# Gated convolution input with tokens on partitions, turned back to channels by three VectorE block transposes a group and quadrant transfers inside SBUF

## The chip, the cores and the metric

The kernel runs on one core of a Trainium2 chip. The metric is device time in microseconds (us), from the first to the last instruction of one execution; "median" is that of several executions. The core has a matrix engine (PE, called TensorE), a vector engine (DVE, VectorE), a scalar engine (ACT, ScalarE), a fourth engine (POOL, GpSimd) and the SyncE queue (SP), which here issues nearly all transfers (DMAs). Each engine works through its own instructions strictly in the order in which the program was built; an instruction that has to wait holds back everything behind it on its engine. The same holds for SP: a transfer that has to wait holds back those behind it.

## What is computed

One layer of a streaming encoder for 384 tokens (256 of a prompt, 8 streams of 16): a normed projection `w_in`, a conformer convolution branch, an attention branch, a gated mix, and a ConvGLU feed-forward part. The part that matters here is the input of the convolution branch and its state:

```python
h = rmsnorm(x, norm_mix_g)
proj = h @ w_in
glu_in = proj[..., :o0]                        # 2 * D_CONV = 2048 columns: values, then gates
u = glu_in[..., :D_CONV] * jax.nn.sigmoid(glu_in[..., D_CONV:])
ext = jnp.concatenate([conv_buf.astype(u.dtype), u], axis=1)
z = layernorm(causal_dwconv(ext, conv_dw_w, conv_dw_b), conv_ln_g, conv_ln_b)
a_out = (z * jax.nn.sigmoid(z)) @ conv_pw_out
new_conv = ext[:, -(CONV_W - 1):]              # the last 30 rows, an output
```

Everything is float32. Each product of the large projections is made of three matmuls on rounded parts ("hi" and "lo" of both factors): hi\*hi, hi\*lo, lo\*hi.

## The kernel before

**Weights.** All weights stream through `ahead` (L205): a raw tile of 256 rows x 512 columns (`raw`, three buffers, L127) is loaded by SP, cast to `hi` by ScalarE (L148) and its remainder `lo` made by VectorE (L149); `hi` and `lo` have three buffers each (L143). So the split of tile j can begin only when PE is through with tile j-3, and the load of tile j only when the split of tile j-3 is done. In the convolution-input columns (GLU) a raw tile holds 256 gate columns and 256 value columns of a group, loaded by two DMAs.

**The GLU stage** (L779) is four jobs ("groups" g = 0..3), each over 16 slices of 128 rows of the model width: 64 *steps* in all, here numbered 0 to 63, two to a weight tile (tile j serves steps 2j and 2j+1; groups end after steps 15, 31, 47 and 63). Jobs are of kind "A" (L243): the weight block is the stationary operand, the activations (384 tokens) are moved, so the result has channels on partitions: four PSUM tiles of 128 channels x 384 tokens, 12 matmuls a step. `glu_evac` (L702) multiplies each by the tokens' norm factors (`rs1b`, the factors as a row repeated on all partitions, built once at L427 to L430 by VectorE and three matmuls), takes the sigmoid on ScalarE and the product on POOL, and leaves `ut` (channels x tokens), which the convolution reads.

**What runs between the steps.** After each step `tick` (L218) advances two side programs. The order of PE's instructions is the program's own order; that of the other engines is decided when the program is built, by the scheduler's estimates and by priorities (`EVAC_AHEAD`, `ATT_AHEAD`).

- *Attention* (`attention`, L678): head h has its operands after step 6+6h (VectorE transposes the cached keys `kc` into `kTs`, L611), its scores after step 9+6h (PE, L622 to L630, the last of them with `kTs`; then a VectorE maximum over each of three score tiles, L636, and the exponentials), its probabilities transposed after step 14+6h, its output made after step 17+6h (PE, L659 to L669, with the cached values `vc`), and a last transpose after step 19+6h. These use three small PSUM tiles in turn (`misc`, L68): the scores take all three, so the output of head h-1, two steps later, needs the maximum of head h's first two score tiles to be done. `load_k` (four DMAs a head), `load_v` and the bias rows `load_b` (four DMAs, and two POOL additions, L603 and L604) are loaded some steps ahead on SP.
- *Convolution* (`conv`, L718): per 128 channels c a `fill` (L729) copies `ut` into an extended buffer, and 31 `tap`s (L747) on VectorE add up the convolution in place. `fill` also makes the new state: two PE transposes (L740, L741), two ScalarE copies and two DMAs.

Of the kernel before, what the change touches and what calls it, by code (L numbers as in the profile page):

```python
# [8 lines left out]
F32 = mybir.dt.float32  # L9
F32R = mybir.dt.float32r  # L10
AF = mybir.ActivationFunctionType
ALU = mybir.AluOpType
# [3 lines left out]
P = 128  # L16
DM = 2048
NT = 384
NTT = 3
# [12 lines left out]
SQ_LAG = 1  # L32
MIX_FIRST, MIX_EVERY = 2, 2
SPLIT_AHEAD, ATT_AHEAD, EVAC_AHEAD = 150, 250, 400

R_FFN, R_DWB, R_LNG, R_LNB, R_FDB, R_QG, R_N = 0, 16, 24, 32, 40, 84, 85
WARM, FILL = 5, 2
# [3 lines left out]
def hybrid_step(  # L41
# [9 lines left out]
    nc = tc.nc  # L51
# [11 lines left out]
    cp, close_cp = pool("consts", side="right")  # L63
# [9 lines left out]
    def misc_tile():  # L73
        return misc.tile([P, 512], F32, tag="misc", name="misc")
# [152 lines left out]
    def gemm(jobs, sides=(), wide=False):  # L227
        for js in jobs:
            js = js if isinstance(js, tuple) else (js,)
            for j in js:  # L230
                nb = 4 if j["kind"] == "A" else NTT
                j["ps"] = [(misc_tile if i == 2 and (wide or j is not js[0]) else acc_tile)() for i in range(nb)]
            for j, k in [(j, k + i) for k in range(0, js[0]["nk"], 2) for j in js for i in range(2)]:
                nb, n, nk, ps = len(j["ps"]), j["n"], j["nk"], j["ps"]
                kk = k % 2
                if kk == 0:
                    ahead(2 if len(plan) > v_last + 3 else 3)
                    hi, lo = ready.pop(0)
                ah, al = j["act"](k)
                st, sp = k == 0, k == nk - 1  # L240
                for m in range(nb):
                    s = slice(m * P, (m + 1) * P)
                    if j["kind"] == "A":  # L243
                        o = ps[m][:, :NT]
                        mm(o, hi[:, kk, s], ah, start=st, stop=False)  # L245
                        mm(o, hi[:, kk, s], al, start=False, stop=False)  # L246
                        mm(o, lo[:, kk, s], ah, start=False, stop=sp)  # L247
                    else:
                        o = ps[m][:, :n]
                        mm(o, ah[:, s], hi[:, kk, :n], start=st, stop=False)  # L250
                        mm(o, ah[:, s], lo[:, kk, :n], start=False, stop=False)  # L251
                        mm(o, al[:, s], hi[:, kk, :n], start=False, stop=sp)  # L252
                if sp:
                    with tc.high_priority(offset=EVAC_AHEAD):
                        for m in range(nb):
                            j["evac"](m, ps[m])
                    if "post" in j:
                        j["post"]()
                    if "done" in j:
                        j["done"]()  # L260
                tick(sides)
# [14 lines left out]
    def job(kind, nk, act, evac, n=512, done=None):  # L276
        d = dict(kind=kind, nk=nk, act=act, evac=evac, n=n)
        if done is not None:
            d["done"] = done
        return d  # L280
# [49 lines left out]
        ready.append(split(*second))  # L330

    rs1 = cp.tile([P, NTT], F32, name="rs1")
    rs1b = cp.tile([P, NT], F32, name="rs1b")

    def diagonals(dg, r):
        for t in range(NTT):
            ts(dg[:, t, :], ident[:], r[:, t:t + 1], None, op0=ALU.mult)
        return dg

    def over_partitions(dg, dst):  # L340
        ps = misc_tile()
        for t in range(NTT):
            mm(ps[:, t * P:(t + 1) * P], ones[:], dg[:, t, :], start=True, stop=True)
        nc.scalar.copy(dst, ps[:, :NT])
# [52 lines left out]
    def first_norm():  # L397
        for c in range(2, 16, 2):
            if c == 2:
                yield  # L400
            yield
            x_chunk(c)
            yield
            x_chunk(c + 1)
            if c % 4 == 2:
                for t in range(NTT):
                    n = c // 4
                    sq = nc.scalar.activation(junk[:], xs[n][:, t, :], AF.Square, accum_out=ssx[:, t, n:n + 1])
                    if c == 14:
                        queued(sq)  # L410
                    else:
                        tc.keep_in_program_order(sq)
            if c < 14:
                yield
            if 2 < c < 14:
                yield
        mt = p_x0.tile([P, NTT], F32, name="mt")
        with tc.high_priority(offset=EVAC_AHEAD):
            nc.vector.tensor_reduce(mt[:], ssx[:], axis=mybir.AxisListType.X, op=ALU.add)
            ts(mt[:], mt[:], 1.0 / DM, EPS, op0=ALU.mult, op1=ALU.add)  # L420
            r = rsqrt(mt[:], [P, NTT], p_x0, "r1")
            nc.vector.tensor_copy(rs1[:], r[:])
        for _ in range(14):
            yield
        small_columns()
        yield
        dg = diagonals(p_x0.tile([P, NTT, P], F32, name="r1d"), rs1)  # L427
        yield
        yield
        over_partitions(dg, rs1b[:])  # L430
        yield


# [263 lines left out]

    ut = p_cv.tile([P, 8, NT], F32, name="ut")

    sgb = [None, None]  # L700

    def glu_evac(g):  # L702
        def ev(m, ps):
            if m < 2:
                sgb[m] = p_att.tile([P, NT], F32, tag="sgb", bufs=2, name="sgb")
                tt(sgb[m][:], ps[:, :NT], rs1b[:], op=ALU.mult)
                nc.scalar.activation(sgb[m][:], sgb[m][:], AF.Sigmoid)
            else:
                u = ut[:, 2 * g + m - 2, :]
                tt(u, ps[:, :NT], rs1b[:], op=ALU.mult)  # L710
                nc.gpsimd.tensor_tensor(u, u, sgb[m - 2][:], op=ALU.mult)
        return ev

    sm = p_cv.tile([P, NT], F32, name="sm")
    sc = p_cv.tile([P, 8, 32], F32, name="sc")
# [2 lines left out]
    def conv():  # L718
        exts = {}

        def load_state(c):
            for a in range(4):
                o = c * P + 32 * a
                d = nc.sync.dma_start(sc[32 * a:32 * a + 30], state_conv[0, :, :, o:o + 32]
                                      .rearrange("b r d -> r b d"))
                if c == 0:
                    queued(d)

        def fill(c):  # L729
            ext = exts[c] = p_cv.tile([P, 24, 46], F32, tag="ext", bufs=2, name="ext")  # L730
            nc.vector.transpose(ext[:, 16:24, 0:32], sc[:])
            u3 = ut[:, c, :].rearrange("p (a t) -> p a t", t=16)
            nc.scalar.copy(ext[:, :, 30:46], u3)
            nc.gpsimd.memset(ext[:, 0, 0:30], 0.0)
            nc.gpsimd.memset(ext[:, 1, 0:14], 0.0)
            nc.scalar.copy(ext[:, 1:16, 14:30], u3[:, 0:15, :])
            nc.scalar.copy(ext[:, 2:16, 0:14], u3[:, 0:14, 2:16])
            su = p_cv.tile([P, 2, P], F32, tag="su", bufs=1, name="su")
            ps = misc_tile()
            tr(ps[:, :P], ut[:, c, 2 * P:], ident[:])  # L740
            tr(ps[:32, P:2 * P], ut[:, c, 224:256], ident[:])  # L741
            nc.scalar.copy(su[:, 0, :], ps[:, :P])
            nc.scalar.copy(su[:32, 1, :], ps[:32, P:2 * P])
            nc.sync.dma_start(sample_conv[0, :, 14:30, c * P:(c + 1) * P], su[:, 0, :])
            nc.sync.dma_start(prompt_conv[0, 0, :, c * P:(c + 1) * P], su[2:32, 1, :])

        def tap(c, w):  # L747
            v = exts[c][:, :, w:w + 16]
            o = ut[:, c, :].rearrange("p (a t) -> p a t", t=16)
            wc = cw[:, w * 8 + c:w * 8 + c + 1]  # L750
            if w == 0:
                ts(o, v, wc, col[:, R_DWB + c:R_DWB + c + 1], op0=ALU.mult, op1=ALU.add)
            else:
                stt(o, v, wc, o, op0=ALU.mult, op1=ALU.add)  # L754
            if w == CW - 1:
                if c == 1:
                    nc.gpsimd.tensor_tensor(sm[:], ut[:, 0, :], ut[:, 1, :], op=ALU.add)
                elif c > 1:
                    nc.gpsimd.tensor_tensor(sm[:], sm[:], ut[:, c, :], op=ALU.add)

        for t in range(-CONV_FIRST, 7 * CONV_LAG + CW):
            for c in range(8):
                w = t - c * CONV_LAG
                if w == -16:
                    load_state(c)
                elif w == -3:
                    fill(c)
                elif 0 <= w < CW:
                    tap(c, w)
            yield  # L770
# [5 lines left out]
    load_b(1)  # L776
    load_v(1)
    att_steps = attention()
    gemm([job("A", 16, ha, glu_evac(g)) for g in range(4)], [att_steps, conv_steps])  # L779
    drain(att_steps)  # L780
    close_att()
    close_qkv()
# [324 lines left out]
```

## Time and profile before

| | |
|---|---|
| median of 3 runs | 1997.92 us (1997.85 to 1998.3) |
| span of the profiled execution, which is its own time | 1996.7 us |
| instructions in it | 24449 |
| GLU stage (first to last matmul at L245 to L247) | 214.4 to 384.6 us, 170.2 us |
| PE busy in it | 167.7 us |
| DVE busy in it | 140.4 us |
| ACT busy in it | 77.9 us |
| POOL busy in it | 17.7 us |
| mean busy share of the 16 DMA engines in it | 64% |

"Busy" is the share of time with an instruction running on the engine. A matmul's own duration is longer than the distance to the next one, since matmuls overlap; the distance between starts is what counts for PE. The "chain" is the profile's walk back from the last instruction to what released it, step by step.

### The profile page before, as it was taken

The numbers are of one execution on the slowest core, as the hardware profiler recorded it, in microseconds if no ns is written. First come the engines' busy times: TensorE is split into PE (matmuls) and PEld (weight loads), VectorE is DVE, ScalarE is ACT, GpSimd is POOL, SyncE is SP. The second block draws the span as 40 slices with busy tenths as digits, with TensorE's granted clock in tenths as the row PEclk, the third lists the DMA queues.
The fourth block names the chain that finished last, engine by engine and source line by source line (L and its number), as shares of the span: only waits on it lengthen the run. The fifth ranks groups of instructions, "written<-read, shape, count | busy, mean of one in ns | idle before, by whom it ended". The sixth has DMA issues, their size and how long they took to land.

```text
span 1996.7 us, 24449 instructions
## 1 busy us (share of the span) xinstructions
PE 1986.5 (99%) x9383; PEld 1676.0 (84%) x9383; DVE 1305.3 (65%) x1908; ACT 743.2 (37%) x1077; POOL 89.5 (4%) x216
## 2 busy tenths in 40 slices
PE   9999999999999999999999999999999999999999
PEld 9888999888888888888888888888888888888887
DVE  4455889788755487676867683377673376638663
ACT  5535354433334433344333432233332233323321
POOL 1000011100000000000000000010000000000000
PEclk9999999999999999999999999999999999999999
DMA  6564767444443334534344443444433444343443
GB/s 184 149 188 117 216 154 161 141 140 131 130 129 124 128 125 163 165 122 137 119 137 126 129 134 129 129 126 127 136 129 132 132 118 137 128 133 120 138 158 106
DMA packets 209254, 275.98 MB, mean 138 GB/s; under 512 B 55878, under 2 KB 96729, under 8 KB 209129
## 3 DMA queue, kind: packets, MB, share of 16 engines
q1 hardware_dynamic: 208817, 273.85, 46.0%
q8 instruction: 73, 1.20, 0.3%
q0 software_dynamic: 288, 0.57, 0.1%
q14 instruction: 44, 0.36, 0.1%
q10 hardware_dynamic: 32, 0.01, 0.0%
HBM read 266.98 MB, written 7.86 MB: 138 GB/s over the span
## 4 chain that ended last, share of the span: by engine, by line
PE 96%; DVE 2%; DMA 1%; issue 0%; SPq 0%; ACT 0%; DVEq 0%; ACTq 0%
PE acc L252 20%; PE acc L250 20%; PE acc L251 20%; PE misc L252 10%; PE misc L251 10%; PE misc L250 10%; PE acc L245 2%; PE acc L247 2%; PE acc L246 2%; DVE lo L149 1%; DMA raw<-in_w_in_dram 0%; DVE mixT L267 0%; DVE ut L754 0%; DMA vc<-in_cache_v_dram 0%; DMA bs<-c_dr 0%
## 5 line engine op out<-in xcount | busy, mean ns | idle before, releaser
L149 DVE TENSOR_TENSOR lo<-raw,hi 128x1024 fp32r<-128x1024 f32 (+2 forms) x481 | 580.5, 1207 | 530.7 <-ACT hi L148 526.8
L148 ACT CAST hi<-raw 128x1024 fp32r<-128x1024 f32 (+2 forms) x481 | 496.3, 1032 | 970.1 <-PE misc L252 841.1
L250 PE MATMUL acc<-hi,xg 128*128 128x512 f32 x704 | 274.9, 390 | 0.0
L252 PE MATMUL acc<-hi,xg 128*128 128x512 f32 x704 | 273.9, 389 | 0.0
L251 PE MATMUL acc<-lo,xg 128*128 128x512 f32 x704 | 273.9, 389 | 0.0
L250 PE MATMUL acc<-hi,hT 128*128 128x512 f32 (+1 forms) x512 | 193.0, 377 | 0.5 <-ACT hT L297 0.5
L252 PE MATMUL acc<-hi,hT 128*128 128x512 f32 (+1 forms) x512 | 190.4, 372 | 0.2
L251 PE MATMUL acc<-lo,hT 128*128 128x512 f32 (+1 forms) x512 | 190.3, 372 | 0.0
L250 PEld LDWEIGHTS acc<-hi,xg 128*128 128x128 f32 x704 | 132.1, 188 | 28.4
L754 DVE SCALAR_TENSOR_TENSOR ut<-ext,cw,ut 128x384 f32<-128x384 f32 x240 | 151.9, 633 | 6.0
L252 PEld LDWEIGHTS acc<-hi,xg 128*128 128x128 f32 x704 | 132.1, 188 | 27.5
L251 PEld LDWEIGHTS acc<-lo,xg 128*128 128x128 f32 x704 | 132.2, 188 | 27.1
L252 PE MATMUL misc<-hi,xg 128*128 128x512 f32 x352 | 137.0, 389 | 0.0
L250 PE MATMUL misc<-hi,xg 128*128 128x512 f32 x352 | 137.0, 389 | 0.0
L251 PE MATMUL misc<-lo,xg 128*128 128x512 f32 x352 | 136.9, 389 | 0.0
L250 PE MATMUL acc<-hi,act 128*128 128x512 f32 x352 | 136.9, 389 | 0.0
L251 PE MATMUL acc<-lo,act 128*128 128x512 f32 x352 | 136.9, 389 | 0.0
L252 PE MATMUL acc<-hi,act 128*128 128x512 f32 x352 | 136.9, 389 | 0.0
L267 DVE STREAM_TRANSPOSE extf<-tok 32x384 f32<-32x384 f32 x176 | 100.3, 570 | 30.9 <-ACT tok L988 28.2
L267 DVE STREAM_TRANSPOSE uT<-tok 32x384 f32<-32x384 f32 x176 | 100.3, 570 | 29.7 <-ACT tok L988 26.9
L250 PEld LDWEIGHTS acc<-hi,hT 128*128 128x128 f32 x512 | 96.2, 188 | 16.1 <-ACT hT L297 1.0
L252 PEld LDWEIGHTS acc<-hi,hT 128*128 128x128 f32 x512 | 96.1, 188 | 15.7 <-DVE hT L298 0.7
(325 smaller groups left out, 3133.8 us busy)
## 6 DMA issues: line engine op xcount, KB each, us to landing
raw<-in_w_up_dram SPq DMA_DIRECT2D x176, 512.0 KB
raw<-in_w_in_dram SPq DMA_DIRECT2D x96, 512.0 KB
raw<-in_w_down_dram SPq DMA_DIRECT2D x88, 512.0 KB
raw<-in_w_in_dram SPq DMA_DIRECT2D x64, 256.0 KB
raw<-in_w_out_dram SPq DMA_DIRECT2D x32, 512.0 KB
raw<-in_w_att_out_dram SPq DMA_DIRECT2D x16, 512.0 KB
raw<-in_conv_pw_out_dram SPq DMA_DIRECT2D x16, 512.0 KB
raw<-in_w_in_dram SPq DMA_DIRECT2D x23, 344.0 KB
```

The source lines that it names most:

```text
L148: queued(nc.scalar.copy(hi[:, k, :o], raw[:, k, :o]), first)
L149: queued(tt(lo[:, k, :o], raw[:, k, :o], f(hi[:, k, :o]), op=ALU.subtract), first)
L245: mm(o, hi[:, kk, s], ah, start=st, stop=False)
L246: mm(o, hi[:, kk, s], al, start=False, stop=False)
L247: mm(o, lo[:, kk, s], ah, start=False, stop=sp)
L250: mm(o, ah[:, s], hi[:, kk, :n], start=st, stop=False)
L251: mm(o, ah[:, s], lo[:, kk, :n], start=False, stop=False)
L252: mm(o, al[:, s], hi[:, kk, :n], start=False, stop=sp)
L267: nc.vector.transpose(put(a, slice(32 * b, 32 * b + 32)), src[32 * a:32 * a + 32, b])
L754: stt(o, v, wc, o, op0=ALU.mult, op1=ALU.add)
```

## The change

The GLU jobs become kind "B": the activations are the stationary operand and 512 weight columns (256 gates, 256 values) are moved, so that tokens are on partitions: three PSUM tiles of 128 tokens x 512 columns, 9 matmuls a step. The norm factor is then one number per partition, and `rs1b` with the work that built it goes away.

```diff
+TURN_AHEAD = 300
-    rs1b = cp.tile([P, NT], F32, name="rs1b")
-        dg = diagonals(p_x0.tile([P, NTT, P], F32, name="r1d"), rs1)
-        yield
-        yield
-        over_partitions(dg, rs1b[:])
-        yield
...
-    sgb = [None, None]
-    def glu_evac(g):
...
+    def glu_job(g):
+        sgt = p_att.tile([P, NTT, 256], F32, tag="sgt", bufs=1, name="sgt")
+        ur = p_att.tile([P, NTT, 256], F32, tag="ur", bufs=1, name="ur")
+
+        def ev(t, ps):
+            nc.scalar.activation(sgt[:, t, :], ps[:, 0:256], AF.Sigmoid, scale=rs1[:, t:t + 1])
+            stt(ur[:, t, :], ps[:, 256:512], rs1[:, t:t + 1], sgt[:, t, :], op0=ALU.mult, op1=ALU.mult)
+
+        def done():
+            tb = p_att.tile([P, 4, 2, NTT, 32], F32, tag="tb", bufs=1, name="tb")
+            with tc.high_priority(offset=TURN_AHEAD):
+                for t in range(NTT):
+                    nc.vector.transpose(tb[:].rearrange("p q m t j -> p t m q j")[:, t],
+                                        ur[:, t, :].rearrange("p (m q j) -> p m q j", m=2, q=4))
+                for a in range(4):
+                    for q in range(4):
+                        nc.sync.dma_start(ut[32 * q:32 * q + 32, 2 * g:2 * g + 2, 96 * a:96 * a + 96],
+                                          tb[32 * a:32 * a + 32, q].rearrange("p m t j -> p m (t j)"))
+            cs = slice(256 * g, 256 * g + 256)
+            nc.sync.dma_start(sample_conv[0, :, 14:30, cs], ur[:, 2, :])
+            nc.sync.dma_start(prompt_conv[0, 0, :, cs], ur[98:128, 1, :])
+
+        return job("B", 16, ha, ev, done=done)
...
-            u3 = ut[:, c, :].rearrange("p (a t) -> p a t", t=16)
-            nc.scalar.copy(ext[:, :, 30:46], u3)
+            u3 = ut[:, c, :].rearrange("p (a t h s) -> p t a h s", a=4, t=NTT, h=2)
+            e3 = ext[:, :, 30:46].rearrange("p (t a h) s -> p t a h s", t=NTT, a=4)
+            for t in range(NTT):
+                nc.scalar.copy(e3[:, t], u3[:, t])
...
-            nc.scalar.copy(ext[:, 1:16, 14:30], u3[:, 0:15, :])
-            nc.scalar.copy(ext[:, 2:16, 0:14], u3[:, 0:14, 2:16])
-            su = p_cv.tile([P, 2, P], F32, tag="su", bufs=1, name="su")
-            ps = misc_tile()
-            tr(ps[:, :P], ut[:, c, 2 * P:], ident[:])
-            tr(ps[:32, P:2 * P], ut[:, c, 224:256], ident[:])
-            nc.scalar.copy(su[:, 0, :], ps[:, :P])
-            nc.scalar.copy(su[:32, 1, :], ps[:32, P:2 * P])
-            nc.sync.dma_start(sample_conv[0, :, 14:30, c * P:(c + 1) * P], su[:, 0, :])
-            nc.sync.dma_start(prompt_conv[0, 0, :, c * P:(c + 1) * P], su[2:32, 1, :])
+            nc.scalar.copy(ext[:, 1:16, 14:30], ext[:, 0:15, 30:46])
+            nc.scalar.copy(ext[:, 2:16, 0:14], ext[:, 0:14, 32:46])
...
-    gemm([job("A", 16, ha, glu_evac(g)) for g in range(4)], [att_steps, conv_steps])
+    gemm([glu_job(g) for g in range(4)], [att_steps, conv_steps])
```

A VectorE transpose turns blocks of 32 x 32 inside a quadrant of 32 partitions; the 16 DMAs per group then move each block row to the quadrant where it belongs (64 runs of 384 bytes each). The state outputs are written straight from `ur`, without PE.

What the scheduler makes of it is seen in the order in which the two programs were built. On VectorE, the weight split that stands last ahead of a head's key transpose (`kTs`), and the step after which that split's buffers are free:

```
scores of head            4 (step 33)   5 (step 39)   6 (step 45)   7 (step 51)
before: last split ahead  tile 16       tile 20       tile 24       tile 28
        free after step   27            35            43            51
after:  last split ahead  tile 18       tile 22       tile 25       tile 28
        free after step   31            39            45            51
```

In the program after, the three evacuations and three transposes of group 1, a copy, the split of tile 18 and four taps stand between the end of step 31 and head 4's key transpose. The maximum of head 4's first score tile stands behind the split of tile 20 (buffers free after step 35) and eight taps that follow that split; head 3's output, after step 35, takes the PSUM tile that this maximum frees.

On SP, behind the load of which weight tile the other loads stand:

```
                                before                  after
16 quadrant transfers           -                       12, 20, 28, 36
last cache_k part, heads 3..7   12, 17, 22, 24, 28      15, 20, 23, 25, 29
bias rows, heads 2..7           10, 14, 19, 23, 25, 29  10, 17, 21, 24, 27, 30
cache_v, heads 2..7             14, 19, 23, 25, 29, 31  17, 21, 24, 27, 30, 31
```

The first part of head 7's cache_k stands ahead of group 2's transfers, the other three stand behind them and behind the load of tile 29.

More of the change, by code (lines that the diff above doesn't have):

```diff
@@ L698, in hybrid_step @@
     ut = p_cv.tile([P, 8, NT], F32, name="ut")
-    sgb = [None, None]
-    def glu_evac(g):
[L703 to L712, printed above, removed]
+    def glu_job(g):
[18 more added lines that the diff above has]
+        return job("B", 16, ha, ev, done=done)
     sm = p_cv.tile([P, NT], F32, name="sm")
```

## The prediction

> **What bounds the kernel now.** First the page's span, busy time and chain, then the busy time of each engine inside the GLU stage.
>
> ```profile
> span 1996.7 us, 24449 instructions
> PE 1986.5 (99%) x9383; PEld 1676.0 (84%) x9383; DVE 1305.3 (65%) x1908; ACT 743.2 (37%) x1077; POOL 89.5 (4%) x216
> PE 96%; DVE 2%; DMA 1%; issue 0%; SPq 0%; ACT 0%; DVEq 0%; ACTq 0%
> ...
> 214.40:384.60 170.20, 167.70 (x1192) 161.52 (x1191) 140.44 (x300) 77.91 (x146) 17.72 (x23) 0.99 0.64 165
> ```
>
> The last row is a window: length, then PE, PEld, DVE, ACT and POOL busy, granted clock, DMA share, GB/s. PE sets the end everywhere: 1986.5 of 1996.7 us. In the GLU stage it lacks 2.5 us, and VectorE, at 140 of 170 us, is close behind it. So two things count: PE work removed, and every wait that makes PE stand. The one wait of the stage, read from the timeline, with the stretch that follows it as a window:
>
> ```profile
> 349.52 0.34 PE L247 MATMUL acc<-hT,lo 128*128 128x384 f32 x1
> 349.70 0.38 PE L622 MATMUL misc<-qt,attT 128*128 128x128 f32 x2
> 349.72 1.04 ACT L148 CAST hi<-raw 128x1024 fp32r<-128x1024 f32 x1 [1.47 <-PE acc L246]
> 350.35 0.38 PE L626 MATMUL misc<-qt,attT 128*128 128x128 f32 x2
> 350.80 1.22 DVE L149 TENSOR_TENSOR lo<-raw,hi 128x1024 fp32r<-128x1024 f32 x1 [1.26 <-ACT hi L148]
> 351.94 1.24 DVE L611 STREAM_TRANSPOSE kTs<-kc 128x1024 f32<-128x1024 f32 x1
> 353.23 0.64 PE L630 MATMUL misc<-kTs,qz 128*32 128x128 f32 x16 [2.50 <-DVE kTs L611]
> 354.46 0.52 PE L245 MATMUL acc<-hT,hi 128*128 128x384 f32 x1
> 354.78 0.52 PE L246 MATMUL acc<-hT,hi 128*128 128x384 f32 x1
> ...
> 354.40:357.80 3.40, 3.40 (x13) 3.40 (x12) 0.48 (x5) 2.23 (x6) 0.00 (x0) 0.50 0.96 290
> ```
>
> Step 51 ends with the first row. Head 7's scores want `kTs` at once, but on VectorE that stands behind the split of tile 28, which may begin only now (tile 25 is done with step 51): hi 1.04, lo 1.2, transpose 1.2, and PE stands 2.50 us. Thereafter the granted clock is 0.50 for 3.4 us: starts lie 320 ns apart instead of 173.5 (below), so 3.4 x (1 - 173.5/320) = 1.6 us are lost too. A wait of 2.5 us costs 4.1. This is the pattern for everything below.
>
> **PE work removed.** Starts of pipelined matmuls in the old form (21 starts from the first row to the second) and in the new form, which a later stage runs already (18 starts):
>
> ```profile
> 291.40 0.33 PE L245 MATMUL acc<-hT,hi 128*128 128x384 f32 x1
> ...
> 294.87 0.34 PE L247 MATMUL acc<-hT,lo 128*128 128x384 f32 x1
> ...
> 450.06 0.39 PE L250 MATMUL misc<-hi,hT 128*128 128x512 f32 x1
> ...
> 453.91 0.39 PE L252 MATMUL acc<-hi,hT 128*128 128x512 f32 x1
> ```
>
> 3.47/20 = 173.5 ns and 3.85/17 = 226.5 ns. 768 x 173.5 = 133.2 becomes 576 x 226.5 = 130.5 us: -2.8. A step falls from 2.08 to 2.04 us.
>
> ```profile
> 542.88 0.39 PE L252 MATMUL misc<-hi,hT 128*128 128x512 f32 x1
> 543.11 0.27 PE L740 MATMUL misc<-ident,ut 128*128 128x128 f32 x1
> ...
> 543.57 0.40 PE L251 MATMUL acc<-lo,hT 128*128 128x512 f32 x1
> ...
> 85.90 0.67 PE misc L343 x6
> ```
>
> Between the outer rows lie two pitches (0.45) and a pair of state transposes: 0.69 - 0.45 = 0.24; eight pairs are -1.8 (rounded down). The three `rs1b` matmuls have no row of their own; the six small ones on the chain took 0.67, more than three can (bounds 0 to 0.67): -0.7. Sum -5.3. If before's wait fell away as well (-4.1), the most that can be gained is -9.4.
>
> **VectorE and SP work added.** Durations in the stage, by line:
>
> ```profile
> L754 DVE SCALAR_TENSOR_TENSOR ut<-ext,cw,ut 128x384 f32<-128x384 f32 x79 | 51.1, 647 | 1.5
> L149 DVE TENSOR_TENSOR lo<-raw,hi 128x1024 fp32r<-128x1024 f32 x33 | 41.3, 1253 | 6.4 <-ACT hi L148 6.3
> L636 DVE CUSTOM_DVE_ANT_0 pr<-misc,bs 128x256 f32<-128x256 f32 (+1 forms) x24 | 8.6, 370 | 2.5 <-PE misc L622 2.2 <-PE misc L630 0.3
> L706 DVE TENSOR_TENSOR sgb<-acc,rs1b 128x384 f32<-128x384 f32 x8 | 4.2, 554 | 0.7 <-PE acc L247 0.7
> L676 DVE COPY attT<-misc 128x128 f32<-128x128 f32 x8 | 2.3, 289 | 6.5 <-PE misc L675 6.5
> L731 DVE STREAM_TRANSPOSE ext<-sc 128x256 f32<-128x256 f32 x4 | 1.7, 434 | 1.5 <-DMA sc<-in_state_conv_dram 1.4
> ```
>
> VectorE in sum hardly changes: 16 x 0.55 = 8.9 us go (L706 and its twin L710), 12 evacuations of 256 columns, which I take at 0.40 (between 0.29 for a copy of 128 columns and 0.65 for a tap of 384), and 12 transposes of 256 columns at 0.43 come: 10. What counts is where they stand: at a group's end, by priority, ahead of everything.
>
> Every wait below is "when VectorE or SP delivers" less "when PE arrives". PE's rows for that are the step (2.04), the scores up to `kTs` (0.87: L622 at 349.70 to the end of the second L626), and these:
>
> ```profile
> 247.65 0.44 PE misc L649 x4
> ...
> 305.74 0.38 PE L659 MATMUL misc<-vt,pT 128*128 128x128 f32 x2
> 307.32 0.42 PE L245 MATMUL acc<-hT,hi 128*128 128x384 f32 x1
> ```
>
> The probabilities' transposes take 0.64 with the one at L652, a head's output 1.6, its last transpose 0.2.
>
> *Head 4's scores (after step 33).* From the end of step 31 VectorE does: the copy behind head 2's last transpose 0.65, three evacuations 1.85, three transposes 3.15, a small copy 3.4, split of tile 18 4.6, four taps 7.0 (0.6 each), `kTs` 8.15. PE arrives at two steps + 0.64 + 0.2 + 0.87 = 5.9. Wait 2.3 (1.6 with evacuations and copies at their shortest, 3.0 at their longest).
>
> *Heads 5 and 6.* `kTs` stands behind splits that begin with the step right before the scores (39, 45), as head 7's did before: 2.5 each.
>
> *Head 3's output (after step 35).* It needs the score tile that head 4's first maximum frees. That stands behind tile 20's split, which begins at the end of step 35 (hi and lo 2.2), and eight taps (4.8), then 0.37: 7.3 us. If the scheduler's order has the maximum free sooner, the lower bound is the values and bias rows of that time, which stand on SP behind group 1's transfers: 4.3; upper 8.
>
> *Head 7's scores.* SP rows:
>
> ```profile
> 230.33 1.41 SPq L724 DMA_DIRECT2D sc<-in_state_conv_dram  x3
> 291.78 0.89 SPq L139 DMA_DIRECT2D raw<-in_w_in_dram  x2
> 337.46 3.21 SPq L587 DMA_DIRECT2D kc<-in_cache_k_dram  x4
> ...
> 324.58 5.33 DMA vc<-in_cache_v_dram
> ```
>
> A small transfer holds SP 0.47 (1.41/3). Sixteen transfers inside SBUF are not in this trace; I take 0.46, between the 0.41 of the fastest issues near them and the 0.61 of the slowest. From the end of step 47: evacuated and turned 2.4; sixteen issues 7.4, so 9.8; tile 29's pair 0.9, 10.7; three `cache_k` parts 1.5, 12.2; landing 4.0 (bounds half of the 5.33 of the four times larger `vc`, 2.7, and 5.3), 16.2; `kTs` 1.2, 17.4. PE arrives after head 5's output 1.6, four steps 8.2, 0.2, 0.64 and 0.87: 11.6. Wait 5.8 (3.4 to 9.6).
>
> The weights themselves survive the block: tile 13's load would land some 15 us after its group's end and is due at step 26, ten steps (20 us) and the heads' work away. The late conv input is no term either: the last tap ends at 569.8, and the first matmul that reads the result of all taps starts only at 612.8.
>
> ```profile
> 569.15 0.62 DVE L754 SCALAR_TENSOR_TENSOR ut<-ext,cw,ut 128x384 f32<-128x384 f32 x1
> 612.76 0.81 PE L813 MATMUL misc<-sm,avg 128*128 128x384 f32 x2
> ```
>
> Without that cover of 43 us each late us of taps would be one at the end.
>
> **Sum.** Waits 2.3 + 2.5 + 2.5 + 7.3 + 5.8 = 20.4. Clock: 1.6 each, certain for the two long waits (3.2), at half for the three others, which are about as long as the one that paid it (2.4): 5.6, bounds 0 and 8. So +26.0 - 9.4 = +16.6: 1996.7 + 16.6 = 2013.3. The median of the runs lies 1.2 above the span: 2014.5.
>
> The Trainium skill, page "TensorE: Matmul & The Clock Gate", section "Part 1: The HAM clock gate (the "warmup" mystery)", has the clock halved only when a whole window of about 3.4 us passed idle. By that rule only the long waits would pay, 3.2 in place of 5.6. The trace does not bear this out: 2.50 us of standing were followed by 3.4 us at 0.50.
>
> **Rivals.**
>
> *A: the removal alone counts.* The waits don't come: an estimated order of a scheduler need not be the order of arrival, and if splits and taps finish one step sooner than I walk them, `kTs` and the maximum are there. It decides if the new waits with their clock sum to less than 9.4; in full, 1997.9 - 9.4 = 1988.5. For it: VectorE has 30 us free in the stage, and six of eight heads wait for nothing today. Against it: the split cannot begin before PE leaves its buffer, and the built order puts `kTs` behind it.
>
> *B: only the VectorE order bites.* Heads 4 to 7 wait for `kTs` as head 7 does now, 2.3 + 3 x 2.5 = 9.8 and clock about 4; the SP block is hidden because PE, held by the earlier waits, arrives later. +13.8 - 9.4 = +4.4: 2002.
>
> *C: the transfers hold SP longer.* 64 runs of 384 bytes each; if sixteen in a row hold SP as the four key loads at 337.46 did (3.21/4 = 0.80 each, against 0.46), a block is 12.8 us instead of 7.4. Head 7 then waits 5.4 more, head 3's output 2 more, the clock 2: about 2024. It decides once an issue takes over some 0.6 us. For it:
>
> ```profile
> DMA packets 209254, 275.98 MB, mean 138 GB/s; under 512 B 55878, under 2 KB 96729, under 8 KB 209129
> ```
>
> Against: a quarter of all packets is that small already, and the stage's DMA share is 0.64.
>
> The Trainium skill, page "DMA: Bandwidth & Descriptors", section "Specifications", wants runs of at least 512 bytes for full rate. The change's runs are below that, and the sum by it would be that of C; nothing in the trace prices such a run inside SBUF.
>
> **How the numbers follow.** Forecast, 2014.5, 0.57; A 0.13; B 0.13; C 0.17. What this kernel's measurement can tell from no change is about 0.2%, 4 us. A is faster (0.13); of B and the forecast's low end, where before's wait is saved and clocks don't drop, 0.09 is no change; slower 0.78. Low end: waits at their low bounds 14.3 with no clock, +4.9, 2002.8, put at 2002 to take in B. High end: 3 + 5 + 8 + 9.6 + 8 - 9.4 = +24.2, 2022. Outside lie A and half of C.
>
> **What would show it.** Right: PE stands at L630 for heads 4 to 7 and at head 3's output (L659 to L664), with 0.5 clock windows behind the long ones; sixteen SP rows of about 0.46 after each group; matmuls of the stage 226 ns apart. Wrong: PE idle in the stage below 9 us; `kTs` done before PE arrives; a wait at the split of weights or at the convolution's end, which I put at nothing; sixteen transfers that hold SP for much over 8 us.

## The result and the profile after

| | before | after |
|---|---|---|
| median | 1997.88 us (4 runs) | 2026.15 us (2023.84 to 2026.35, 4 runs) |
| span of the profiled execution | 1996.7 us | 2024.1 us |
| GLU stage, first matmul to last | 170.2 us | 199.4 us |

The ratio is 1.0141 (95% interval 1.013 to 1.0153): slower, as forecast, but 4 us beyond the top of the stated range of 2002 to 2022. First the page of after, then the stage as a window (length, busy time of PE, PEld, DVE, ACT and POOL, granted clock, DMA share, GB/s), then what PE waited for:

```profile
span 2024.1 us, 24071 instructions
PE 1988.8 (98%) x9169; PEld 1652.3 (82%) x9169; DVE 1293.4 (64%) x1913; ACT 742.6 (37%) x1080; POOL 82.4 (4%) x208
PE 93%; DVE 4%; DMA 1%; SPq 1%; issue 0%; ACT 0%; DVEq 0%; ACTq 0%
```

```profile
213.13:412.55 199.42, 171.88 (x994) 138.74 (x993) 143.17 (x318) 80.33 (x153) 10.87 (x18) 0.93 0.57 149
```

```profile
PE misc L625 <- DVE kTs L606: 16.4, 4, 9.3
PE misc L654 <- DVE mx L631: 10.1, 1, 10.1
...
PE misc L658 <- DMA vc<-in_cache_v_dram: 1.0, 2, 0.7
PE acc L252 <- DVE lo L150: 0.8, 1, 0.8
```

Columns of the last: total us, times, longest. Nearly all lies in the GLU stage. The four waits for `kTs` are the scores of heads 4 to 7 (1.81, 2.67, 2.67 and 9.25 us), the 10.1 us and 0.75 us more are head 3's output. So all five waits of the forecast came, at their places. Of the eight key transposes only one stood for its keys, head 7's:

```profile
DVE kTs L606 <- DMA kc<-in_cache_k_dram: 6.5, 1, 6.5
```

At heads 4 to 6 the keys were there in time, and the transpose stood where the built order has it, behind a split (at head 4 behind four taps as well). The chain shows SPq, which had 0% before, at 1%.

Around head 3's output the timeline reads:

```profile
295.23 10.23 SPq L711 DMA_DIRECT2D ut<-tb  x16
...
304.67 0.39 PE L253 MATMUL acc<-hi,hT 128*128 128x512 f32 x1
...
307.31 4.32 DVE L753 SCALAR_TENSOR_TENSOR ut<-ext,cw,ut 128x384 f32<-128x384 f32 x8
...
308.10 0.64 SPq L595 DMA_DIRECT2D bs<-d_dr  x1
308.84 0.40 SPq L587 DMA_DIRECT2D vc<-in_cache_v_dram  x1
...
314.01 0.72 POOL L598 TENSOR_TENSOR bs<-bs,mk 128x256 f32<-128x256 f32 x1 [31.84 <-DMA bs<-c_dr]
314.77 0.29 DVE L631 CUSTOM_DVE_ANT_0 pr<-misc,bs 128x128 f32<-128x128 f32 x1 [3.14 <-POOL bs L598]
315.12 0.80 PE L654 MATMUL misc<-vt,pT 128*128 128x128 f32 x2 [10.07 <-DVE mx L631]
...
316.67 1.08 PE L658 MATMUL misc<-vc,pz 128*32 128x128 f32 x16 [0.75 <-DMA vc<-in_cache_v_dram]
```

Sixteen transfers hold SP for 10.23 us, 0.64 each. The bias rows go out behind them and land 5 us later; VectorE is through with its eight taps at 311.63 and then stands 3.14 us for them. Head 7's scores:

```profile
359.33 0.38 PE L654 MATMUL misc<-vt,pT 128*128 128x128 f32 x2
...
361.55 10.59 SPq L711 DMA_DIRECT2D ut<-tb  x16
...
372.23 1.04 SPq L140 DMA_DIRECT2D raw<-in_w_in_dram  x2
373.32 2.42 SPq L582 DMA_DIRECT2D kc<-in_cache_k_dram  x3
...
378.94 1.25 DVE L606 STREAM_TRANSPOSE kTs<-kc 128x1024 f32<-128x1024 f32 x1 [6.49 <-DMA kc<-in_cache_k_dram]
...
380.24 1.08 PE L625 MATMUL misc<-kTs,qz 128*32 128x128 f32 x16 [9.25 <-DVE kTs L606]
```

And the granted clock (the 0.50 or 1.00) behind the waits for the scores of heads 4, 5, 6 and 7, and in the last row behind that of head 3's output:

```profile
300.70:304.10 3.40, 3.40 (x19) 2.81 (x16) 3.40 (x8) 0.00 (x0) 0.00 (x0) 1.00 0.15 36
334.00:337.00 3.00, 3.00 (x9) 2.35 (x8) 1.40 (x10) 0.49 (x2) 1.51 (x3) 0.50 0.99 202
354.40:357.40 3.00, 3.00 (x8) 2.31 (x7) 0.42 (x4) 1.68 (x4) 0.00 (x0) 0.50 0.41 88
...
381.25:384.60 3.35, 3.35 (x12) 2.69 (x9) 1.96 (x4) 0.15 (x1) 0.00 (x0) 0.50 0.49 128
315.10:318.50 3.40, 2.63 (x22) 1.92 (x23) 3.28 (x14) 1.75 (x7) 0.74 (x4) 0.50 1.16 297
```

Four of the five waits were paid a second time in lowered clock; the 1.81 us wait was not. Behind the two waits of 2.67 us, which ended at 332.21 and 352.94, the clock fell only 1.2 to 1.5 us later: the windows 332 to 334 and 353 to 354.4 still have 0.92.

### The profile page after: what moved, and what is told of

The parts are those of the page before. It is cut to its first block, busy times and chain, and to the rows that moved or that the text cites. A ratio compares the mean times of both kernels' runs of the same rounds, so it can differ in the third digit from the quotient of the medians.

```text
span 2024.1 us, 24071 instructions
## 1 busy us (share of the span) xinstructions
PE 1988.8 (98%) x9169; PEld 1652.3 (82%) x9169; DVE 1293.4 (64%) x1913; ACT 742.6 (37%) x1080; POOL 82.4 (4%) x208
## 4 chain that ended last, share of the span: by engine, by line
PE 93%; DVE 4%; DMA 1%; SPq 1%; issue 0%; ACT 0%; DVEq 0%; ACTq 0%
PE acc L251 21%; PE acc L253 21%; PE acc L252 21%; PE misc L251 9%; PE misc L253 9%; PE misc L252 9%; DVE ut L753 1%; DVE lo L150 1%; DMA raw<-in_w_in_dram 1%; DMA vc<-in_cache_v_dram 0%; DVE mixT L268 0%; SPq L711 0%; ACT hi L149 0%; PE misc L625 0%; DMA kc<-in_cache_k_dram 0%
## 5 line engine op out<-in xcount | busy, mean ns | idle before, releaser
L251 PE MATMUL acc<-hi,hT 128*128 128x512 f32 (+1 forms) x704 | 273.1, 388 | 0.0
L252 PE MATMUL acc<-lo,hT 128*128 128x512 f32 (+1 forms) x704 | 267.8, 380 | 0.8 <-DVE lo L150 0.8
L253 PE MATMUL acc<-hi,hT 128*128 128x512 f32 (+1 forms) x704 | 267.5, 380 | 0.2
L251 PEld LDWEIGHTS acc<-hi,hT 128*128 128x128 f32 x704 | 133.6, 190 | 25.1 <-issue 1.9
L253 PEld LDWEIGHTS acc<-hi,hT 128*128 128x128 f32 x704 | 133.6, 190 | 24.1 <-DVE hT L299 0.7
L252 PEld LDWEIGHTS acc<-lo,hT 128*128 128x128 f32 x704 | 133.7, 190 | 23.5 <-DVE lo L150 1.6
L753 DVE SCALAR_TENSOR_TENSOR ut<-ext,cw,ut 128x384 f32<-128x384 f32 x240 | 138.9, 626 | 1.0
```

## The experiments

The theory after this reading: the time is lost on SP. A transfer inside SBUF holds it 0.64 us, sixteen in a row 10.3, and keys, bias rows and values behind them come late; the order of VectorE's work is only built around that. The rivals: VectorE's three evacuations and three turns at a group's end; the traffic of the small runs on the DMA engines; the taps ahead of the maximum. All runs are compared with the kernel before on the same chip; medians lie about 1 to 3 us above the profiled spans, and PE's first wait at the kernel's start differs by up to 1.5 us from one execution to the next.

### Moving the quadrants without DMAs

```diff
-    nc.sync.dma_start(ut[32 * q:32 * q + 32, ...], tb[32 * a:32 * a + 32, q]...)
+    nc.gpsimd.tensor_copy(ut[32 * q:32 * q + 32, ...], tb[32 * a:32 * a + 32, q]...)
```

> The sixteen quadrant transfers of a group become sixteen GpSimd copies, so SP is not held; group ends on VectorE and the matmul form stay. If the SP block is the cause (theory): head 3's output no longer waits; by the built order only the key transposes of heads 6 and 7 still stand behind a split that begins with the step before their scores, so two waits of about 2.7 us with 1.8 us of lowered clock each remain: 1996.7 - 9.4 + 9.0 = about 1996 profiled, median about 1997.5 (half the waits: 1992). If the three evacuations and three turns on VectorE are the cause (rival): the waits stay and it is above 2020. A third way: GpSimd copies cost so much that the convolution is late and PE waits at its end; then over 2000 with a wait at the layer norm's first matmul.

Profiled 1997.2 us, ratio 1.0008 (0.9999 to 1.0018). What PE waited for in the stage:

```profile
PE misc L625 <- DVE kTs L606: 5.3, 2, 2.7
...
PE misc L621 <- DVE pz L648: 1.0, 1, 1.0
```

Two waits of 2.67 us, at heads 6 and 7, and nothing at head 3's output: 27 us gone with the transfers, while evacuations and turns stayed. The VectorE rival falls. The 1.0 us was not expected.

### Keys earlier, bias rows earlier

```diff
-  kc ... bufs=2        load_k(d["h"] + 1)  after head_operands
+  kc ... bufs=3        load_k(d["h"] + 2)  after head_operands; load_k(1) at the start
```

> After, with each head's four key loads issued one head earlier (a third key buffer); transfers stay on SP. Theory (keys late on SP, and for that reason late in VectorE's order): waits at the scores of heads 4 to 7 (1.8, 2.7, 2.7, 9.25 us) and their lowered clock (about 6) go, head 3's output with 10.1 stays: about 2024 - 22.5 = 2001.5 profiled, median 2003. Rival (VectorE's group ends set these waits): heads 4 to 6 keep theirs and only head 7's goes: about 2013.

Profiled 2019.8 us, ratio 1.0121 (1.0106 to 1.0136): neither number. The waits:

```profile
PE misc L654 <- DVE mx L631: 23.3, 4, 12.5
...
PE misc L658 <- DMA vc<-in_cache_v_dram: 1.1, 2, 0.9
```

No wait for `kTs` is left, at any head: the keys' place on SP was the cause of all four. At head 7 the keys had come late. At heads 4 to 6 they had not; there the earlier loads let the scheduler build the transposes earlier (head 4's at 284.77 instead of 298.79, head 5's at 300.39 instead of 330.92), with the group's end on VectorE unchanged. But head outputs now wait for a maximum, and the time is back (12.5 at head 3, 7.5 at head 6). At head 3 VectorE has eleven taps ahead of it and then stands 4.0 us for bias rows. The same for the bias rows alone (third `bs` buffer, `load_b` one head earlier):

> After, with each head's bias rows loaded one head earlier (a third buffer); keys and transfers as they were. If head 3's output waited for the bias rows, in fact and in the built order (theory): its 10.8 us of waiting and some 2 us of lowered clock go, head 7's 9.25 us stay: about 2011 profiled, median 2013. If it waited for the taps ahead of the maximum on VectorE whatever the rows do (rival): 3 us at most go, 2021.

Profiled 2026.6 us, ratio 1.0151 (1.0136 to 1.0166):

```profile
PE misc L625 <- DVE kTs L606: 17.4, 3, 9.4
PE misc L658 <- DMA vc<-in_cache_v_dram: 10.9, 1, 10.9
```

The wait for the maximum is gone. With the rows early the scheduler also put it ahead of the split and the taps (it runs at 301.02), so the rows' place on SP set both, and this run doesn't part them; in after, split and taps took 6.7 of the 10.07 us and the rows the last 3.1. Nothing is gained: head 3's output now stands 10.9 us for `vc`, the next transfer on SP behind the block. Whichever load stands there is waited for.

### The same place in the kernel before

The keys' edit in the kernel before:

> The kernel before with each head's key loads one head earlier. If its one wait (2.50 us at head 7's scores and 1.6 us of lowered clock) came from keys that stand late: 1996.7 - 4.1 = 1992.6 profiled, median 1993.8. If it came from VectorE's load: no change, 1998.

Profiled 1992.6 us, median 1994.44, ratio 0.9985 (0.9975 to 0.9994), with no wait in the stage. The old wait too came from the keys' place. They were not late in fact: VectorE never stood for keys in the stage of before. With the earlier loads head 7's transpose is built ahead of the split (336.52 instead of 351.94).

And the block alone, added to the kernel before (its result is used by nobody):

```diff
+  nc.gpsimd.tensor_copy(tb[:, :, 0, 0, 0:1], ut[:, 2 * g + 1, 0:4]...)
+  16 x nc.sync.dma_start(tz[32 * q:32 * q + 32, :, 96 * a:96 * a + 96], tb[32 * a:32 * a + 32, q]...)
```

> The kernel before, with sixteen such transfers added on SP at each group's end, from a tile that holds zeros to one that nobody reads; a small GpSimd copy makes them wait for the group. Matmul form, evacuations and outputs stay. If the SP block alone makes the waits (theory): some 10 us at head 3's output, 9 at head 7's scores and 2 at head 4's, with 5 us of lowered clock, in place of before's 4.1: about 2018 profiled, median 2019. If VectorE's new work at the group's end is needed for them (rival): below 2005.

Profiled 2033.9 us, ratio 1.0191 (1.0177 to 1.0205):

```profile
PE misc L630 <- DVE kTs L611: 17.0, 4, 9.7
PE misc L659 <- DVE mx L636: 10.0, 1, 10.0
PE misc L663 <- DMA vc<-in_cache_v_dram: 4.0, 2, 2.6
```

The block makes the waits without a single new VectorE instruction. The size was underestimated by 16 us: values came late at two more places, and heads 5 and 6 waited 4.6 and 2.4 us for their keys' transposes.

### Letting the loads overtake

```diff
+  with tc.high_priority(offset=300):   # around load_k, load_b and load_v
```

> After, with one thing changed: the key, value and bias loads of a head may overtake the sixteen transfers on SP (the same priority as these). No transfer is removed and none is made faster. If only what stands behind the block counts (theory): the waits of heads 3 to 7 go and what is left is the removal of PE work and of before's wait, 1996.7 - 9.4 = 1987.3 profiled, median 1989; up to 5 us more if weights now wait. If the block itself, the transfers' traffic or VectorE's group ends cost the time (rival): above 2010.

Profiled 2038.7 us, ratio 1.0219 (1.0205 to 1.0233), slower than after. No head waits any more; PE waits for weights:

```profile
PE acc L251 <- ACT hi L149: 34.7, 3, 17.7
PE acc L252 <- DVE lo L150: 9.8, 3, 6.3
```

```profile
252.05 10.39 SPq L712 DMA_DIRECT2D ut<-tb  x16
262.54 0.53 SPq L592 DMA_DIRECT2D bs<-c_dr  x1
...
265.30 6.12 SPq L582 DMA_DIRECT2D kc<-in_cache_k_dram  x4
271.46 3.25 SPq L140 DMA_DIRECT2D raw<-in_w_in_dram  x5
```

Nine more loads with priority make the block 19 us long (252.05 to 271.46), and the weights are now what stands behind it. Both expectations miss: the number is the rival's, the mechanism is the theory's with another victim. The prediction had said that the weights survive a block of 7.4 us; they survive 10.3 (after), and not 19.

### Same bytes, another queue; and the dose

```diff
-  nc.sync.dma_start(ut[32 * q:...], tb[32 * a:...])
+  nc.gpsimd.dma_start(ut[32 * q:...], tb[32 * a:...])
```

> After, with the same 64 transfers issued by GpSimd's queue instead of SP's: same bytes, same runs, same DMA engines. If SP's issue time is the cost (theory): head 3's output and head 7 stop waiting; by the built order the keys of heads 5 to 7 stand ahead of the late splits or nearly so, with at most the 2.7 us of two heads: 1988 to 1997 profiled. If the small runs load the DMA engines so that other loads land late (rival): it stays above 2010.

Profiled 1994.8 us; median 1998.05, ratio 1.0003 (0.9994 to 1.0013). The two waits are at heads 6 and 7, 2.67 us each; the windows are the 3.4 us behind each:

```profile
PE misc L625 <- DVE kTs L606: 5.3, 2, 2.7
```

```profile
334.20:337.60 3.40, 3.40 (x28) 2.73 (x29) 1.59 (x12) 2.81 (x9) 0.00 (x0) 1.00 1.03 232
...
353.30:356.70 3.40, 3.38 (x22) 2.50 (x23) 2.63 (x5) 2.14 (x4) 0.00 (x0) 0.50 0.59 169
```

The same runs of 384 bytes over the same DMA engines make PE wait for no load when SP is free, and the two waits that are left go with earlier keys (last run below): the traffic rival falls. The Trainium skill, page "DMA: Bandwidth & Descriptors", section "Specifications", asks for runs of 512 bytes or more; short as the runs are, they are not what was paid here. Then with four (block row and target quadrant the same), and with eight (target quadrants 1 and 3), of sixteen on GpSimd's queue:

> After, with four of the sixteen transfers of a group (those that stay in their quadrant) issued by GpSimd's queue: twelve at 0.64 us hold SP for 7.7 us, about the 7.4 that the prediction took for sixteen at 0.46. If the price of an issue is the step that failed (theory): head 3's output waits 7.3 to 8 instead of 10.8, head 7's scores about 6.6 instead of 9.25, heads 5 and 6 2.67 each as before, head 4 0 to 1.8: 2016 to 2019 profiled. If the lateness of the loads has nothing to do with the number of transfers on SP (rival): 2022 or more.

Profiled 2016.6 us, ratio 1.0099 (1.0085 to 1.0112):

```profile
PE misc L625 <- DVE kTs L606: 12.7, 3, 7.4
PE misc L658 <- DMA vc<-in_cache_v_dram: 8.0, 1, 8.0
```

Twelve transfers hold SP for 7.8 to 8.7 us in the first three groups, a little more than the 7.4 that the prediction took for sixteen, and the two long waits come out at 8.0 and 7.4 us, near its 7.3 and 5.8; head 4 waits for nothing. At head 3's output the agreement is in part luck: three of the four bias loads now stand ahead of the block (from 290.17), and PE waits for values instead of the maximum.

> After, with eight of sixteen transfers on GpSimd's queue: SP held for 5.1 us. Theory: head 3's output waits 4.5 to 6 (VectorE's splits and taps may then be what is late), head 7's scores about 4, heads 5 and 6 at most 2.67: 2005 to 2012 profiled. If the wait has a threshold, not a slope (rival): as with twelve, or as with none (1995).

Profiled 2008.7 us, ratio 1.0065 (1.0051 to 1.0079). Head 3's output no longer waits, since its bias rows and values were built ahead of the block (290.70 to 293.24); heads 5, 6 and 7 wait 7.4, 2.7 and 4.4 us for `kTs`. Head 5's 7.4, expected at 2.67 at most, is the built order of VectorE, which does not stand for keys there but has a split and seven taps ahead:

```profile
314.84 1.22 DVE L150 TENSOR_TENSOR lo<-raw,hi 128x1024 fp32r<-128x1024 f32 x1
...
315.98 4.54 DVE L753 SCALAR_TENSOR_TENSOR ut<-ext,cw,ut 128x384 f32<-128x384 f32 x7
...
320.43 1.24 DVE L606 STREAM_TRANSPOSE kTs<-kc 128x1024 f32<-128x1024 f32 x1
...
321.73 0.65 PE L625 MATMUL misc<-kTs,qz 128*32 128x128 f32 x8 [7.38 <-DVE kTs L606]
```

So the total met the range and its terms did not. SP, too, was held longer than the 5.1 us in one group: 8.78 us in group 1, where one of the eight issues took 2.92. In profiled spans 16, 12, 8 and 0 transfers on SP give 2024.1, 2016.6, 2008.7 and 1994.8: 1.7 to 2.0 us for each transfer of a group. The total falls with every step, but each run has a built order of its own, and it is not one wait that shrinks: whether any single wait has a slope or a threshold is not shown.

### What an issue costs

> The kernel before with sixteen transfers inside SBUF added on SP at each group's end, between tiles that nothing else uses, in four shapes: 32 partitions x 768 bytes in one run; 32 x 384 in one run; 16 x 768 in one run; 32 x 4 runs of 192 bytes. Only the time that an issue holds SP is read. If it goes by the number of runs or bytes (theory): the first three below the 0.64 of 32 x 2 runs, towards 0.46, and the last above. If every transfer inside SBUF costs 0.64 whatever its shape (rival): all four alike.

SP's rows for the four shapes, in the order of the expectation:

```profile
252.08 11.13 SPq L727 DMA_DIRECT2D tz<-tb  x16
...
297.83 10.06 SPq L729 DMA_DIRECT2D tz<-tb  x16
...
363.07 10.08 SPq L731 DMA_DIRECT2D tz<-tb  x16
...
418.26 12.69 SPq L733 DMA_DIRECT2D tz<-tb  x16
```

Half the bytes, half the partitions: still 0.63 us each. The first row has one issue of 1.58 us in it and the last one of 3.22; the other fifteen of each take 0.63 from start to start like those of the middle rows. The fourth shape did not become what was meant: the trace has no packet of 192 bytes, its packets are of 768, so it repeats the first. All four are alike and the rival holds, for one and two runs a partition; whether more runs cost more is not shown. An issue inside SBUF is above the 0.46 of a weight or key load here, and the size does not lower it. It is not alone in that: the bias load `d_dr` held SP 0.64 in after, too. Why, no run shows.

### A version below both

GpSimd copies and early keys together, then GpSimd's queue and early keys:

> Quadrant moves by GpSimd copies (as in the first experiment) and keys one head earlier: the two waits of 2.67 us at the scores and their clock go, about 1997.2 - 9 = 1988 profiled, median 1989.5, below both kernels. If it stays at 1997, these waits were not the keys' place.

Profiled 1992.6 us, median 1995.62, ratio 0.9989 (0.998 to 0.9998): below before, not by what was expected. The two waits are gone, but four small ones (0.6 to 1.2 us) stand in the stage, for VectorE.

> After, with all transfers on GpSimd's queue and each head's keys loaded one head earlier: of the run with the queue alone the two waits of 2.67 us and 1.6 us of lowered clock go: 1994.8 - 6.9 = 1988 profiled, median about 1990.5, below both kernels. If the keys' place isn't what makes these two waits: 1995.

Profiled 1989.3 us, median 1991.88, ratio 0.9969 (0.9956 to 0.9981). Its stage:

```profile
213.22:378.91 165.69, 164.01 (x995) 133.56 (x994) 146.16 (x326) 80.90 (x153) 35.08 (x65) 1.00 0.66 174
```

164.0 us of PE work with the clock at full, one wait of 1.7 us. With its transfers off SP and the keys early, the changed kernel is 6 us faster than the kernel before. Against the kernel before with early keys (0.9985, in another batch) the intervals just overlap, so how much the new matmul form adds to that edit is not settled by the medians.

## Why the prediction was wrong

| term, us | predicted | measured |
|---|---|---|
| head 4's scores | 2.3 | 1.81 |
| scores of heads 5 and 6 | 2.5 + 2.5 | 2.67 + 2.67 |
| head 3's output (maximum, then values) | 7.3 | 10.07 + 0.75 |
| head 7's scores | 5.8 | 9.25 |
| head 6's output (values) | 0 | 0.26 |
| lowered clock | 5.6 | 7.9 |
| next stage's first weights | 0 | 0.75 |
| removed | -9.4 | -8.8 |
| sum | +16.6 | +27.4 |

Clock is what is left of the stage: 199.42 - 27.48 of waiting - 164.0 (PE's work in the last run). Removed is what is left of the sum; two executions without the old wait, the last run less its 1.7 and the kernel before with early keys, give 1987.6 and 1992.6, so 5.0 for the forms and transposes against the 5.3 predicted, each from one execution.

**The step that failed is a size: "Sixteen transfers inside SBUF are not in this trace; I take 0.46, between the 0.41 of the fastest issues near them and the 0.61 of the slowest."** They take 0.64 from start to start, above both ends, so a block lasted 10.2 to 10.6 us in the first three groups instead of 7.4. From that follows more than half of the miss of 10.8 us: some 3.0 at head 7's scores and 2.8 at head 3's output, and part of the clock behind them. At head 7's scores the prediction's walk from the end of step 47 has the block end at 9.8 us; it ended at 372.14 - 359.33 = 12.8. The transpose ended 3.5 us late (20.9 against 17.4), and PE arrived when it was said to (11.7 against 11.6). With sixteen transfers cut to twelve the total comes near the forecast's (2016.6 against 2013.3).

**At head 3's output the same size changed which of two lines was last.** The VectorE walk was right: the taps ended 6.7 us after the end of step 35, the prediction's 7.0. It had put the bias rows at the lower end (4.3); behind a block 2.8 us longer, and with 5 us to land, they came 3.1 us after the taps. Had the block been those 2.8 us shorter, they would have come 0.3 us after the taps (an estimate from these rows), near the forecast. The bound of 8 for this wait held only VectorE's side, so the range had no room for it.

**The clock was paid more often than half.** Both waits of 2.67 us halved it, and behind the long ones it stayed at 0.50 for longer than the 3.4 us that the prediction counted (4.4 us behind head 7's, 380.30 to 384.70). The sum ended at the upper bound (7.9 against 8.0).

**What "VectorE's order" meant was half right.** The waits of heads 4 to 6 came at the forecast size and in the forecast way: the transpose stands behind a split, and the keys are there. But that it stands there comes from the keys' place on SP, as early keys show, and not from the group's end on VectorE, which those runs keep. Nor is it the block's doing alone: with the block off SP two heads still waited 2.67 us each, and the kernel before had such a wait without any block.

Rival C gave the nearest time, 2024, and its condition (an issue over 0.6 us) was met, though not its reason: issues were evenly 0.64, not held up like the key loads at 0.80.

Two slips in the working changed nothing: PE's arrivals at the scores of heads 4 and 7 add up to 5.8 and 11.5, not 5.9 and 11.6, and in the kernel before seven heads of eight, not six, waited for nothing.

**Right:** the sign, the five places, PE's removed work, the hidden convolution end. The weights were nearly right: the fourth group's block cost the next stage 0.75 us.

## What to carry over

On an in-order DMA queue the price of new transfers is their issue time, paid again for every load behind them that PE then waits for: count the issues, measure one, and look for the load that is due next, then the one after it. Moving one late load earlier handed most of the wait to the next; taking the block to a queue with nothing urgent behind it took away every wait for a load, and the two waits that were left went with earlier keys. The Trainium skill, page "DMA: Bandwidth & Descriptors", section "Issuing engine by pattern", gives simple transfers to SyncE; in this kernel what is queued there decides, and GpSimd's queue was 29 us better by the profiled spans (1994.8 against 2024.1) and 28 by the medians.

## What the runs showed of the hardware

An issue inside SBUF held SP for 0.63 to 0.64 us, start to start, with 384 to 768 bytes in one or two runs a partition, on 32 partitions or on 16; a few single issues took 1.6 to 3.2 us. And equal waits are not paid equally: in one execution a wait of 2.67 us was followed by 3.4 us at clock 1.00 and another of 2.67 us by 3.4 us at 0.50 (the run with GpSimd's queue). The Trainium skill, page "TensorE: Matmul & The Clock Gate", section "Part 1: The HAM clock gate (the "warmup" mystery)", has a free-running window of 3413 ns, by which the phase of a wait would matter; that fits. That a whole idle window is needed does not: waits of 2.50 and 2.67 us were enough.
